# Recurrent mixer with five gate projections one iteration earlier and modulation rows in its last iterations; both MLPs with the second product's first weights loaded third

## The chip, the cores and the metric

The kernel runs on one core of a Trainium2 chip. The metric is the device time of one execution in microseconds (us); the time before is the median of three runs. One further execution was recorded by the hardware profiler, and all rows below are from it. The engines are PE (matrix products), DVE, ACT, POOL and SP; in this kernel SP only issues transfers, and POOL issues some and does a few sums.

## The reference, cut to what matters

The kernel computes a trunk of two layers on one sequence of 1024 frames and 1024 channels. Layer A is a recurrent mixer and an MLP, layer B an attention and an MLP. The change touches the mixer and both MLPs:

```python
def recurrent_mixer(hn, w_in, ...):
    z = hn @ w_in                                  # 1024 -> 2 x 1408
    gate, xr = jnp.split(z, 2, axis=-1)
    xr = causal_depthwise_conv(xr, conv_w, conv_b) # width 4
    y = rg_lru(xr, ...)                            # 16 blocks of 88 channels
    return (y * jax.nn.gelu(gate)) @ w_out
...
    r = sigmoid(einsum(xb, w_a) + b_a); i = sigmoid(einsum(xb, w_x) + b_x)
    log_a = -8.0 * r * softplus(-lam); a = exp(log_a)
    u = sqrt(-expm1(2.0 * log_a)) * (i * x)
    h[s] = a[s] * h[s - 1] + u[s]                  # along the sequence
...
def sqrelu_mlp(hn, w1, w2):
    return jnp.square(jax.nn.relu(hn @ w1)) @ w2
...
    mod = c_act @ ada_w[layer] + ada_b[layer]      # six vectors that modulate a layer
```

## The kernel before, in words

**Products.** Every product is made in three passes (`mm3`, L329 to L331) from operands that are split into a high part (a rounded copy, made by ACT, L196) and a low part (the rest, made by DVE, L200): low part by weights' high, high by weights' low, high by high. So each weight and each operand costs an ACT and a DVE instruction before PE can use it.

**The stream.** A planner (`Stream`) holds one list of all weights, modulation rows and MLP operands. `load` sends the transfers in the list's order through SP's queue (L159) into seven staging slots (`ws`); a slot comes free when its last split has run. Instructions are emitted in program order, with a hand-made clock of *ticks*: `at(d, f)` puts a job d ticks later. A projection unit (`proj2`) has four ticks, a block of `gates` one. Each engine works through its own instructions strictly in the order in which they were emitted.

**The mixer.** `w_in` gives 22 units of 128 channels: 11 of `xr` (unit t) and 11 of `gate` (unit 11 + t). A unit is 48 matmuls: two halves of 512 frames by 8 chunks by 3 passes. `xr(t)` runs a unit; ACT scales it into two tiles (L912, L914); `conv(t)` is three DVE steps (L919). One tick later `copies` moves the rows of tile t into tiles of one 88-channel block each by transfers that POOL issues (L927); `split_hi` (ACT, L933) and `split_lo` (DVE, L940) follow after 5 and 6 ticks for tiles 3 to 9. `_done(t)` lists the blocks that are complete with tile t: 4 is [5, 6], 7 is [10], 8 is [11, 12]. `recur` runs the blocks of a tile: `gates` (12 matmuls of 88 rows each, sigmoids on ACT, L966; the product i·x on DVE, L971), `tanhs` and `roots` (ACT, the last step is L986), and for each block `scan` and `scan2` on DVE (L990, L991, L992, L996, L997). `ycopy` sends the result to tiles of 128 channels (POOL, L1004), `gated` multiplies it with the GELU of the gate (DVE, L1010), and SP stores it. Iteration t of the loop (4 to 10) is `xr(t)`, `recur(_done(t - 1))`, `gate(t - 1)`. So PE goes: ... xr 4, block 4, gate 3, xr 5, blocks 5 and 6, gate 4, xr 6, block 7, gate 5, ... xr 8, block 10, gate 7, xr 9, blocks 11 and 12, gate 8, xr 10, block 13, gate 9, gate 10, blocks 14 and 15.

**Modulation rows.** `some(n)` puts n rows of `ada_w` into the list. Each is one load of 512 KB and one DVE instruction (L362) that reduces it into a vector.

**The MLPs.** Both products go by seven products for each 2 by 2 block (`PROD`: B11, T1, T2, B22, B21, T3, T4 name the combinations of the hidden operand; `quads.step` runs them). The first product's results are stored to `hid` by ACT's queue, their differences are formed on DVE (L1174), and the second product reads them back as operands. Its weights come as *quads*: four loads of 256 KB in three of the seven slots, four sums on DVE (L126; on POOL from the third quad on), then the splits. At its first step (`s == 0`) the list holds six loads of operands (B11, T1 and T2, two loads each), then the first quad, then the other operands. The results are added into `h` on DVE (L1278), which frees the bank; L1256 adds in the first product.

Of the kernel before, what the change touches and what calls it, by code (L numbers as in the profile page):

```python
# [18 lines left out]
NT = 11  # L19
# [284 lines left out]
def trunk(ctx: ExitStack, tc: tile.TileContext, I, out, dbg=None, stop=None):  # L304
# [103 lines left out]
    gate_item(_done(0) + _done(1))  # L408
    w_in(2)
    gate_item(_done(2))  # L410
    for t in range(4, NT):
        w_in(NT + t)
        some({4: 3, 6: 3, 8: 2}.get(t, 0))
        gate_item(_done(t - 1))
        w_in(t - 1)
    w_in(NT - 1)
    gate_item(_done(NT - 1))
    ygd = dp.tile([NT, 128, S], F32, name="ygd")
# [55 lines left out]
    def mlp_units(l):  # L474
        for f in range(4):
            ws.add(I["w1"][l][f], 1024)
        for q in range(2, 16):
            u, v = I["w1"][l][2 * q], I["w1"][l][2 * q + 1]
            ws.add_quad(u[:, :512], u[:, 512:], v[:, :512], v[:, 512:], 512, V)
            ada_late(0 if l or q == 2 else 2 if q in (3, 15) else 3)  # L480
        for s in STEPS[: 16 if l else 15]:
            c = slice(s * 128, s * 128 + 512)
            if s == 0:

                for nm in NAMES[:3]:
                    hid_item(l, [(0, nm), (1, nm)])
                    hid_item(l, [(2, nm), (3, nm)])
            ws.add_quad(*(I["w2"][l][s % 4][x][:, c] for x in range(4)), 512, G if s > 1 else V)
            if s == 0:
                for nm in NAMES[3:]:  # L490
                    hid_item(l, [(0, nm), (1, nm)])
                    hid_item(l, [(2, nm), (3, nm)])
            if l or s < 14:
                if s < 15:
                    for nms in HLOADS:
                        hid_item(l, [(s + 4, nm) for nm in nms])
        if l == 0:
            for e in range(2):
                ws.add(I["w2t"][e], 1024)
            hid_item(l, [(18, "B11"), (18, "B12")])  # L500
            hid_item(l, [(18, "B22"), (18, "B21")])
            hid_item(l, [(16, "B12"), (17, "B12")])
            hid_item(l, [(15, "B12")])
# [392 lines left out]
    at = ws.at  # L896
# [47 lines left out]
    def conved(t):  # L944

        conv(t)
        at(1, copies, t)
        late = 2 < t < NT - 1
        at(5 if late else 3, split_hi, t)
        at(6 if late else 4, split_lo, t)  # L950

    gunit = [None]

# [106 lines left out]
    recur(_done(0) + _done(1))  # L1060
    gate(2)
    recur(_done(2))
    for t in range(4, NT):
        xr(t)
        recur(_done(t - 1))
        gate(t - 1)
    ws.cap["a"] = 14
    gate(NT - 1)
    recur(_done(NT - 1))
# [739 lines left out]
```

## Time and profile before

| | us |
|---|---|
| median of 3 runs (lowest to highest) | 2373.84 (2373.54 to 2380.44) |
| the profiled execution | 2376.3 |
| its span | 2374.5 |
| PE busy | 2276.8 (96%) |
| DVE busy | 1751.4 (74%) |
| ACT busy | 1242.1 (52%) |
| mean granted clock of PE | 0.988 of full |

PE is busy for nearly the whole span, so the time follows PE: it is the sum of PE's work at the clock that was granted, and of its idle time. The rows below are read in this way: a view of 50 us stretches shows where PE is idle or slow, the waits name who ended the idle time, and the timelines of the other engines show why that one was late. The granted clock is 1.00 at 2.4 GHz and 0.50 at 1.2 GHz; a stretch with both has a mean between. "Busy" of PE is longer at half the clock for the same work.

### The profile page before, as it was taken

How to read it: one execution, taken by the hardware profiler on the slowest of the kernel's cores; microseconds unless marked ns; L12 is line 12 of the kernel's file. 1: busy time of each engine (PE TensorE's matmuls, PEld its weight loads, DVE VectorE, ACT ScalarE, POOL GpSimd, SP SyncE). 2: the span in 40 equal slices, each digit the busy share in tenths (PEclk: the TensorE clock that was granted, in tenths of full speed). 3: DMA queues.
4: the chain of work that ended last, by engine and by line, in shares of the span. 5: the costliest groups of instructions: out<-in, count | busy, mean ns of one | idle time of the engine just before them, and what ended most of it. 6: DMA issues, size and time to landing. Idle time of an engine off the chain costs nothing.

```text
span 2374.5 us, 31723 instructions
## 1 busy us (share of the span) xinstructions
PE 2276.8 (96%) x11740; PEld 1932.3 (81%) x11740; DVE 1751.4 (74%) x2580; ACT 1242.1 (52%) x2051; POOL 398.9 (17%) x419
## 2 busy tenths in 40 slices
PE   4998999999999899999999999999999999999999
PEld 2876777878887677888999999998888888778887
DVE  8687779588787777777774638997386665777775
ACT  5596783275554533434433229996175555634342
POOL 0000100000000023330000048874000000033322
PEclk9998999999999999999999999999999999999999
DMA  8333339326666865546344200014214444865543
GB/s 317 93 110 118 112 110 345 115 72 239 239 246 228 287 236 150 157 140 223 109 141 134 80 10 13 10 43 138 76 40 177 160 160 171 292 236 161 153 148 135
DMA packets 141639, 363.46 MB, mean 153 GB/s; under 512 B 14924, under 2 KB 17100, under 8 KB 141484
## 3 DMA queue, kind: packets, MB, share of 16 engines
q1 hardware_dynamic: 113756, 278.45, 35.2%
q10 hardware_dynamic: 23824, 71.44, 8.0%
q0 software_dynamic: 3904, 11.54, 1.9%
q8 instruction: 92, 1.51, 0.3%
q14 instruction: 63, 0.52, 0.1%
HBM read 260.19 MB, written 89.65 MB: 147 GB/s over the span
## 4 chain that ended last, share of the span: by engine, by line
PE 66%; DVE 11%; DMA 10%; ACT 7%; issue 4%; POOL 1%; ACTq 0%; SPq 0%; DVEq 0%; POOLq 0%
PE b L330 20%; PE b L331 20%; PE b L329 20%; DMA hid<-s 5%; DMA ws<-in_w_dram 3%; DVE wl L200 2%; PE b L1615 2%; ACT s L1585 1%; DVE s L200 1%; DVE s L1174 1%; ACT s L334 1%; DMA ws<-hid 1%; POOL ws L126 1%; PE b L1634 1%; PE b L1635 1%
## 5 line engine op out<-in xcount | busy, mean ns | idle before, releaser
L329 PE MATMUL b<-s,wh 128*128 128x512 f32 (+1 forms) x2532 | 1000.5, 395 | 33.9 <-DVE s L1278 7.1
L330 PE MATMUL b<-s,wh 128*128 128x512 f32 (+1 forms) x2532 | 995.4, 393 | 19.3 <-DVE s L940 10.4
L331 PE MATMUL b<-s,wl 128*128 128x512 f32 (+1 forms) x2296 | 903.3, 393 | 4.7 <-DVE wl L200 4.7
L329 PEld LDWEIGHTS b<-s,wh 128*128 128x128 f32 (+1 forms) x2532 | 478.3, 189 | 150.3 <-ACT wh L196 10.0
L330 PEld LDWEIGHTS b<-s,wh 128*128 128x128 f32 (+1 forms) x2532 | 478.5, 189 | 125.3 <-DVE s L940 10.8
L196 ACT ACTIVATE wh<-ws 128x1024 fp32r<-128x1024 f32 (+2 forms) x302 | 290.7, 972 | 481.7 <-POOL ws L126 250.2
L331 PEld LDWEIGHTS b<-s,wl 128*128 128x128 f32 (+1 forms) x2296 | 434.1, 189 | 101.7 <-DVE wl L200 7.5
L200 DVE TENSOR_TENSOR wl<-ws,wh 128x1024 fp32r<-128x1024 f32 (+2 forms) x249 | 304.8, 1227 | 133.3 <-ACT wh L196 131.1
L1278 DVE SCALAR_TENSOR_TENSOR s<-b,mod,s 128x512 f32<-128x512 f32 x221 | 164.5, 745 | 86.3 <-PE b L331 86.2
L200 DVE TENSOR_TENSOR s<-ws,s 128x512 fp32r<-128x512 f32 x284 | 224.2, 807 | 0.0
L126 POOL TENSOR_TENSOR ws<-ws 128x512 f32<-128x512 f32 x21 | 27.7, 1319 | 1144.7 <-DMA s<-hsp 463.8
L329 PE MATMUL b<-wh,s 128*128 128x256 f32 x768 | 216.5, 284 | 0.0
L331 PE MATMUL b<-wh,s 128*128 128x256 f32 x768 | 215.2, 283 | 0.9 <-DVE s L580 0.9
L330 PE MATMUL b<-wl,s 128*128 128x256 f32 x768 | 215.9, 283 | 0.0
L196 ACT ACTIVATE s<-ws 128x512 fp32r<-128x512 f32 x284 | 164.0, 618 | 55.0 <-DMA ws<-hid 22.2
L331 PEld LDWEIGHTS b<-wh,s 128*128 128x128 f32 x768 | 146.5, 192 | 1.4 <-DVE s L580 1.3
L329 PEld LDWEIGHTS b<-wh,s 128*128 128x128 f32 x768 | 147.1, 192 | 0.3 <-issue 0.2
L330 PEld LDWEIGHTS b<-wl,s 128*128 128x128 f32 x768 | 147.0, 192 | 0.3 <-issue 0.2
L362 DVE CUSTOM_DVE_ANT_0 ws<-ws,cb,vec 128x1024 f32<-128x1024 f32 x59 | 75.2, 1280 | 74.9 <-DMA ws<-in_ada_dram 72.2
L1256 DVE TENSOR_TENSOR s<-s,b 128x512 f32<-128x512 f32 x84 | 57.3, 683 | 73.4 <-PE b L331 66.9
L1254 ACT ACTIVATE s<-b 128x512 f32<-128x512 f32 x84 | 50.1, 596 | 90.5 <-PE b L331 89.3
L1385 ACT ACTIVATE s<-b 128x256 f32<-128x256 f32 x96 | 31.6, 387 | 122.4 <-PE b L331 110.8
(165 smaller groups left out, 3066.3 us busy)
## 6 DMA issues: line engine op xcount, KB each, us to landing
hid<-s ACTq DMA_DIRECT2D x128, 512.0 KB, 5.1
ws<-hid SPq DMA_DIRECT2D x118, 512.0 KB, 4.8
ws<-in_w_dram SPq DMA_DIRECT2D x220, 256.0 KB, 3.7
ws<-in_ada_dram SPq DMA_DIRECT2D x56, 512.0 KB, 4.4
s<-in_ada_dram SPq DMA_DIRECT2D x40, 512.0 KB, 9.1
ws<-in_w_in_dram SPq DMA_DIRECT2D x22, 512.0 KB, 5.9
hsp<-s SPq DMA_DIRECT2D x32, 256.0 KB, 2.0
s<-hsp SPq DMA_DIRECT2D x16, 512.0 KB, 6.3
```

The source lines that it names most:

```text
L126: eng.tensor_tensor(out=out, in0=in0, in1=in1, op=op)
L196: self.nc.scalar.activation(out=hi[:rows, :n], in_=src, func=AF.Copy)
L200: self.nc.vector.tensor_tensor(out=lo[:rows, :n], in0=src, in1=hi[:rows, :n].bitcast(F32), op=ALU.subtract)
L329: PE.matmul(ps, ah, bh, start=start, stop=False, skip_group_check=more)
L330: PE.matmul(ps, ah, bl, start=False, stop=False, skip_group_check=more)
L331: return PE.matmul(ps, al, bh, start=False, stop=stop, skip_group_check=more).ins
L362: V.tensor_tensor_reduce(out=t, in0=t, in1=cb, op0=ALU.mult, op1=ALU.add, scale=1.0, scalar=bias, accum_out=dst)
L1254: A_.activation(out=t, in_=ps, func=AF.Copy)
L1256: V.tensor_tensor(out=t, in0=t, in1=ps, op=ALU.add)
L1278: V.scalar_tensor_tensor(out=t, in0=ps, scalar=g2[:, m : m + 1], in1=t, op0=ALU.mult, op1=ALU.add)
L1385: A_.activation(out=d, in_=ps[:, :, e * 128 : (e + 1) * 128], func=AF.Copy)
L1615: PE.transpose(ps[:, x, e * 128 : (e + 1) * 128], ptile[e][:, col : col + 128], ident)
```

## The change

**The mixer.** The unit `gate(3)` runs ahead of the loop, and iteration t runs `gate(t)` for t = 4 to 7 (tiles 3 to 7, five units, each one iteration earlier), none at t = 8, and `gate(t - 1)` at t = 9 and 10 as before. The list of weights follows. The splits of the converted rows come after 4 and 5 ticks instead of 5 and 6, and after 3 and 4 for tile 8. The modulation rows are listed at iterations 8, 9 and 10 (3, 2, 3) instead of 4, 6 and 8 (3, 3, 2).

**The MLPs.** At `s == 0` the first quad stands behind the two loads of B11, ahead of those of T1 and T2.

```diff
@@ the list of weights, mixer
     w_in(2)
     gate_item(_done(2))
+    w_in(3)
     for t in range(4, NT):
         w_in(NT + t)
-        some({4: 3, 6: 3, 8: 2}.get(t, 0))
+        some({8: 3, 9: 2, 10: 3}.get(t, 0))
         gate_item(_done(t - 1))
-        w_in(t - 1)
+        if t != 8:
+            w_in(t if t < 8 else t - 1)
@@ mlp_units
             if s == 0:
 
-                for nm in NAMES[:3]:
+                for nm in NAMES:
                     hid_item(l, [(0, nm), (1, nm)])
                     hid_item(l, [(2, nm), (3, nm)])
-            ws.add_quad(*(I["w2"][l][s % 4][x][:, c] for x in range(4)), 512, G if s > 1 else V)
-            if s == 0:
-                for nm in NAMES[3:]:
-                    hid_item(l, [(0, nm), (1, nm)])
-                    hid_item(l, [(2, nm), (3, nm)])
+                    if nm == "B11":
+                        quad(0)
+            else:
+                quad(s)
@@ conved
-        late = 2 < t < NT - 1
-        at(5 if late else 3, split_hi, t)
-        at(6 if late else 4, split_lo, t)
+        late = 2 < t < NT - 1 and t != 8
+        at(4 if late else 3, split_hi, t)
+        at(5 if late else 4, split_lo, t)
@@ the loop
     recur(_done(2))
+    gate(3)
     for t in range(4, NT):
         xr(t)
         recur(_done(t - 1))
-        gate(t - 1)
+        if t != 8:
+            gate(t if t < 8 else t - 1)
```

In the changed kernel the lines that are named here stand five or seven further down: L919 is L924, L933 is L938, L940 is L945, L971 is L976, L990 to L992 are L995 to L997, L996 and L997 are L1001 and L1002, L1010 is L1015.

**First place: DVE ahead of the low splits of blocks 5 and 6.** Before (the two L940 rows read the blocks' tiles s_1135 and s_1138; L990 to L997 are the scan of block 4, L200 the low split of a weight, L1010 is `gated`):

```order
L1010 TENSOR_TENSOR s_704<-s_704,s_1045 128x1024
L990 SCALAR_TENSOR_TENSOR s_1116<-s_1085,s_1116 88x1024
L991 SCALAR_TENSOR_TENSOR s_1085<-s_1085,s_1114 88x1024
L992 TENSOR_SCALAR s_1085<-s_1085 88x1024
L996 TENSOR_TENSOR s_1116<-s_1116,s_856 88x1024
L997 SCALAR_TENSOR_TENSOR s_1114<-s_1085,s_1116 88x1024
L200 TENSOR_TENSOR wl_1212<-ws_777,wh_1211 128x1024
L940 TENSOR_TENSOR s_1233<-s_1135,s_1207 88x1024
L940 TENSOR_TENSOR s_1235<-s_1138,s_1209 88x1024
```

Now (s_1184 and s_1187 are the tiles of blocks 5 and 6; L924 is the convolution of tile 4, from which they are copied, L976 the i·x of block 4):

```order
L924 SCALAR_TENSOR_TENSOR s_1094<-s_1093,vec,s_1094 128x1023
L924 SCALAR_TENSOR_TENSOR s_1094<-s_1093,vec,s_1094 128x1022
L924 SCALAR_TENSOR_TENSOR s_1094<-s_1093,vec,s_1094 128x1021
L200 TENSOR_TENSOR wl_1162<-ws_748,wh_1161 128x1024
L976 TENSOR_TENSOR s_847<-s_1140,s_847 88x1024
L995 SCALAR_TENSOR_TENSOR s_1168<-s_1139,s_1168 88x1024
L996 SCALAR_TENSOR_TENSOR s_1139<-s_1139,s_1166 88x1024
L997 TENSOR_SCALAR s_1139<-s_1139 88x1024
L945 TENSOR_TENSOR s_1252<-s_1184,s_1229 88x1024
L945 TENSOR_TENSOR s_1254<-s_1187,s_1231 88x1024
L1001 TENSOR_TENSOR s_1168<-s_1168,s_847 88x1024
L1002 SCALAR_TENSOR_TENSOR s_1166<-s_1139,s_1168 88x1024
```

The two low splits have moved from behind the last two steps of block 4's scan and a weight's low split to between its third and fourth steps.

**Second place: DVE ahead of the low splits of blocks 11 and 12.** Before, from the second step of tile 8's convolution on (L990 to L997 are the scan of block 10, s_1712 its tile; the L940 rows read s_1911 and s_1914, the tiles of blocks 11 and 12):

```order
L919 SCALAR_TENSOR_TENSOR s_1821<-s_1820,vec,s_1821 128x1022
L919 SCALAR_TENSOR_TENSOR s_1821<-s_1820,vec,s_1821 128x1021
L200 TENSOR_TENSOR wl_1889<-ws_1398,wh_1888 88x704
L971 TENSOR_TENSOR s_1712<-s_1867,s_1712 88x1024
L990 SCALAR_TENSOR_TENSOR s_1895<-s_1866,s_1895 88x1024
L991 SCALAR_TENSOR_TENSOR s_1866<-s_1866,s_1893 88x1024
L992 TENSOR_SCALAR s_1866<-s_1866 88x1024
L996 TENSOR_TENSOR s_1895<-s_1895,s_1712 88x1024
L997 SCALAR_TENSOR_TENSOR s_1893<-s_1866,s_1895 88x1024
L200 TENSOR_TENSOR wl_1980<-ws_1461,wh_1979 128x1024
L940 TENSOR_TENSOR s_2001<-s_1911,s_1975 88x1024
L940 TENSOR_TENSOR s_2003<-s_1914,s_1977 88x1024
```

Now, from the last step of block 9's scan on (s_1764 is the tile of block 10, s_1970 and s_1973 are those of blocks 11 and 12):

```order
L1002 SCALAR_TENSOR_TENSOR s_1772<-s_1742,s_1776 88x1024
L1015 TENSOR_TENSOR s_1444<-s_1444,s_1678 128x1024
L924 SCALAR_TENSOR_TENSOR s_1880<-s_1879,vec,s_1880 128x1023
L924 SCALAR_TENSOR_TENSOR s_1880<-s_1879,vec,s_1880 128x1022
L924 SCALAR_TENSOR_TENSOR s_1880<-s_1879,vec,s_1880 128x1021
L200 TENSOR_TENSOR wl_1948<-ws_1595,wh_1947 128x1024
L976 TENSOR_TENSOR s_1764<-s_1926,s_1764 88x1024
L945 TENSOR_TENSOR s_2025<-s_1970,s_2007 88x1024
L945 TENSOR_TENSOR s_2027<-s_1973,s_2009 88x1024
L995 SCALAR_TENSOR_TENSOR s_1954<-s_1925,s_1954 88x1024
```

The two low splits have moved from behind the scan of block 10 and a second weight split to right behind block 10's i·x; between tile 8's convolution and them two instructions of DVE are left of eight. On PE the unit `gate(7)`, which stood between xr 8 and these blocks, is gone from there.

**Third place: SP at the start of the first MLP's second product.** Before (one row per load; x2 is two):

```order
L159 DMA ws_5527<-hid 128x2x512
L159 DMA ws_5569<-hid 128x2x512
L159 DMA ws_5573<-hid 128x2x512
L159 DMA ws_5613<-hid 128x2x512
L159 DMA ws_5663<-hid 128x2x512
L159 DMA ws_5703<-hid 128x2x512
L159 DMA ws_5707<-in_w_dram 128x512
L159 DMA ws_5740<-in_w_dram 128x512
L159 DMA ws_5763<-in_w_dram 128x512 x2
L159 DMA ws_5770<-hid 128x2x512
```

Now:

```order
L159 DMA ws_5527<-hid 128x2x512
L159 DMA ws_5569<-hid 128x2x512
L159 DMA ws_5573<-in_w_dram 128x512
L159 DMA ws_5662<-in_w_dram 128x512
L159 DMA ws_5702<-in_w_dram 128x512 x2
L159 DMA ws_5707<-hid 128x2x512
L159 DMA ws_5735<-hid 128x2x512
L159 DMA ws_5741<-hid 128x2x512
L159 DMA ws_5769<-hid 128x2x512
L159 DMA ws_5773<-hid 128x2x512
```

The four loads of weights have moved from the seventh place to the third, and the four loads of T1's and T2's operands behind them. DVE's instructions follow: the sums and the splits of the first weights now stand ahead of the low splits of T1 and T2. The second MLP has the same pieces in the same order.

## Rows read from the trace of the kernel before

**Rows 1.** The page, part 1: busy time, share of the span and instructions of PE.

```profile
PE 2276.8 (96%) x11740; PEld 1932.3 (81%) x11740; DVE 1751.4 (74%) x2580; ACT 1242.1 (52%) x2051; POOL 398.9 (17%) x419
```

**Rows 2.** Stretches of 50 us: busy time and instructions of PE, weight loads, DVE, ACT and POOL; then the granted clock of PE, the share that the transfer engines were busy, and GB/s.

```profile
150.00:200.00 50.00, 39.63 (x149) 30.01 (x148) 45.58 (x39) 35.51 (x43) 6.33 (x12) 0.80 0.46 137
800.00:850.00 50.00, 41.23 (x146) 31.61 (x147) 43.75 (x65) 27.91 (x46) 0.26 (x1) 0.83 0.88 314
```

**Rows 3.** Waits of PE over the whole span: who ended them, us in total, times, and the longest.

```profile
PE b L330 <- DVE s L940: 10.4, 1, 10.4
...
PE b L329 <- ACT wh L196: 7.0, 4, 2.8
PE b L329 <- ACT s L196: 5.7, 2, 2.9
...
PE b L331 <- DVE wl L200: 4.7, 5, 1.4
```

**Rows 4.** Timeline of PE in the mixer, start and duration of single matmuls (a matmul starts before the one ahead of it has ended), and in brackets the idle time ahead and its releaser.

```profile
169.67 0.39 PE L330 MATMUL b<-s,wh 128*128 128x512 f32 x1
...
174.20 0.40 PE L329 MATMUL b<-s,wh 88*88 88x512 f32 x1
184.98 0.73 PE L330 MATMUL b<-s,wh 88*88 88x512 f32 x1 [10.37 <-DVE s L940]
```

**Rows 5.** The stretch behind that wait, columns as in rows 2.

```profile
185.00:197.50 12.50, 12.50 (x30) 8.36 (x31) 11.08 (x11) 8.01 (x11) 0.55 (x1) 0.50 0.68 211
```

**Rows 6.** Timelines of ACT and DVE: the high splits of blocks 5 and 6, the end of block 1's scan, and the low splits of blocks 5 and 6 (start, duration).

```profile
168.49 2.01 ACT L933 ACTIVATE s<-s 88x1024 fp32r<-88x1024 f32 x2
...
150.25 2.29 DVE L997 TENSOR_TENSOR_SCAN s<-s,s 88x1024 f32<-88x1024 f32 x1
...
183.71 2.35 DVE L940 TENSOR_TENSOR s<-s,s 88x1024 fp32r<-88x1024 f32 x2
```

**Rows 7.** Timelines of ACT and DVE from the gates of blocks 8 and 9 to the convolution of tile 8.

```profile
248.54 2.42 ACT L966 ACTIVATE s<-b,vec 88x512 f32<-88x512 f32 x4
...
257.65 2.19 ACT L986 ACTIVATE s<-s,sp 88x1024 f32<-88x1024 f32 x2
259.75 1.04 ACT L933 ACTIVATE s<-s 88x1024 fp32r<-88x1024 f32 x1
...
258.84 1.22 DVE L990 SCALAR_TENSOR_TENSOR s<-s,s 88x1024 f32<-88x1024 f32 x1 [6.63 <-ACT s L986]
...
261.95 1.22 DVE L940 TENSOR_TENSOR s<-s,s 88x1024 fp32r<-88x1024 f32 x1
...
267.67 1.22 DVE L990 SCALAR_TENSOR_TENSOR s<-s,s 88x1024 f32<-88x1024 f32 x1
...
274.24 1.20 DVE L1010 TENSOR_TENSOR s<-s,s 128x1024 f32<-128x1024 f32 x1
275.35 3.91 DVE L919 SCALAR_TENSOR_TENSOR s<-s,vec,s 128x1023 f32<-128x1023 f32 x3
279.18 0.88 DVE L200 TENSOR_TENSOR wl<-ws,wh 88x704 fp32r<-88x704 f32 x1
```

**Rows 8.** The copies of blocks 11 and 12: their issue on POOL, and the transfers issued from 279 to 281 (KB each, us from issue to landing).

```profile
279.83 1.02 POOL L927 DMA_DIRECT2D s<-s  x2 [3.93 <-issue]
...
s<-s POOLq DMA_DIRECT2D x1, 352.0 KB, 5.7
s<-s POOLq DMA_DIRECT2D x1, 128.0 KB, 3.5
```

**Rows 9.** The first MLP at the start of its second product: timelines of SP (time from the first issue to the end of the last of a row), DVE and PE.

```profile
763.28 25.94 SPq L159 DMA_DIRECT2D ws<-hid  x6
789.46 4.48 SPq L159 DMA_DIRECT2D ws<-in_w_dram  x4
...
789.35 4.90 DVE L200 TENSOR_TENSOR s<-ws,s 128x512 fp32r<-128x512 f32 x8
799.61 0.69 DVE L126 TENSOR_TENSOR ws<-ws 128x512 f32<-128x512 f32 x1 [5.37 <-DMA ws<-in_w_dram]
...
816.34 0.74 DVE L1278 SCALAR_TENSOR_TENSOR s<-b,mod,s 128x512 f32<-128x512 f32 x1
...
801.45 0.62 PE L329 MATMUL b<-s,wh 128*128 128x512 f32 x1 [2.81 <-ACT wh L196]
...
817.23 0.47 PE L329 MATMUL b<-s,wh 128*128 128x512 f32 x1 [2.93 <-ACT s L196]
...
831.90 0.50 PE L329 MATMUL b<-s,wh 128*128 128x512 f32 x1 [1.90 <-ACT wh L196]
```

**Rows 10.** Stretches there, columns as in rows 2.

```profile
801.45:808.50 7.05, 6.00 (x14) 4.20 (x15) 7.02 (x11) 6.29 (x11) 0.00 (x0) 0.52 0.90 299
...
806.00:831.00 25.00, 20.90 (x78) 16.02 (x76) 22.25 (x35) 15.03 (x27) 0.00 (x0) 0.88 0.94 334
```

**Rows 11.** The second MLP at the same place: timelines of DVE and PE, and one stretch.

```profile
2042.44 0.69 DVE L126 TENSOR_TENSOR ws<-ws 128x512 f32<-128x512 f32 x1 [2.26 <-DMA ws<-in_w_dram]
...
2059.17 0.74 DVE L1278 SCALAR_TENSOR_TENSOR s<-b,mod,s 128x512 f32<-128x512 f32 x1
...
2060.06 0.47 PE L329 MATMUL b<-s,wh 128*128 128x512 f32 x1 [2.81 <-ACT s L196]
...
2048.00:2072.00 24.00, 21.19 (x87) 17.06 (x86) 22.35 (x36) 15.64 (x28) 0.00 (x0) 0.93 0.96 342
```

More of the change, by code (lines that the diff above doesn't have):

```diff
@@ L481, in mlp_units, with quad @@
         for s in STEPS[: 16 if l else 15]:
-            c = slice(s * 128, s * 128 + 512)
+            def quad(s):
+                c = slice(s * 128, s * 128 + 512)
+                ws.add_quad(*(I["w2"][l][s % 4][x][:, c] for x in range(4)), 512,
+                            G if s > 1 else V)
             if s == 0:
-                for nm in NAMES[:3]:
+                for nm in NAMES:
                     hid_item(l, [(0, nm), (1, nm)])
                     hid_item(l, [(2, nm), (3, nm)])
-            ws.add_quad(*(I["w2"][l][s % 4][x][:, c] for x in range(4)), 512, G if s > 1 else V)
-            if s == 0:
-                for nm in NAMES[3:]:
-                    hid_item(l, [(0, nm), (1, nm)])
-                    hid_item(l, [(2, nm), (3, nm)])
+                    if nm == "B11":
+                        quad(0)
+            else:
+                quad(s)
             if l or s < 14:
```

## The prediction

> **What bounds the kernel now.** The page's first part comes first: PE is busy for 2276.8 of 2374.5 us [rows 1], so a change of this size can only gain where PE is idle or slow. The 50 us stretches then show two such places that the change touches: 150 to 200, where PE has 39.63 us of work at a mean clock of 0.80, and 800 to 850, with 41.23 at 0.83 [rows 2]. The waits of PE say who ended the idle time: in the mixer one wait of 10.4 us on a low split (L940); in the MLPs the high splits of weights (7.0 in four waits), the low splits of weights (4.7 in five) and the high splits of operands (5.7 in two) [rows 3].
>
> *The mixer.* PE's first matmul of block 5 starts at 174.20, the second, which reads the low part, at 184.98 [rows 4]. From 185.0 to 197.5 the clock is 0.50 and PE is busy for all of 12.50 us [rows 5]: at the full level that work is 6.25 us, so the wait costs 10.37 + 6.25 = **16.6 us**. The high splits were done at 170.5, the low ones began at 183.71 [rows 6]: DVE, which runs its list in order, was still at older scans. Its backlog is the cause, not data that came late.
>
> *The MLPs.* In the first one PE waits 2.81 us ahead of B11, 2.93 ahead of T2 and 1.90 ahead of the second quad [rows 9]. Behind the first of these the mean clock is 0.52 over 7.05 us [rows 10], some 3.4 us lost. DVE sat idle for 5.37 us until the last load of the first quad had landed (799.61) [rows 9].
>
> **The mixer, step by step.** A unit of 48 matmuls takes 10.9 us: 20 of them start in 4.53 us (169.67 to 174.20) [rows 4]; the 12 of a block take 2.7. PE takes up xr 4 at about 138.6 (counted back from 174.20 by xr 5, gate 3, block 4 and xr 4). In its place comes `gate(3)`, whose weights now stand at xr 4's place in the list, so they come when xr 4's came. Counting on from 138.6: gate 3 to 149.5, xr 4 to 160.4, block 4 to 163.1, gate 4 to 174, xr 5 to **185**. Blocks 5 and 6 are wanted 10.8 us later than before.
>
> *When are they ready?* Block 1's scan ends at 152.5 [rows 6]; ahead of its end the order is nearly the same. DVE then has, up to the end of tile 4's convolution: two scans of 6.57 (267.67 to 274.24), two `gated` of 1.1, two weight splits of 1.1 and a convolution of 3.83 [rows 7]: 152.5 + 13.1 + 2.2 + 2.2 + 3.8 = 173.8. The copies follow 0.65 later on POOL (279.18 to 279.83) and land after 3.5 to 5.7 [rows 7, 8]; a high split is 1.04 and a low split 1.1 [rows 7]. Together: 180 to 182. Slack is 3 to 5 us, so the stall and its slow clock should go: **+16.6**. The moved modulation rows help here, as none stands ahead of these splits now; I put them at nothing elsewhere: in DVE's new list they lie between blocks 5 and 6 and block 8's scan, a stretch in which DVE had gaps (the last of 6.63 us before 258.84 [rows 7]). If that cover failed, eight of some 1.3 would cost up to 10.
>
> *What is next.* One gate unit is now ahead, and it is used up at tile 8, whose iteration has none. PE after: blocks 8 and 9 from 236.9 to 242.4 (5.7 earlier than before), gate 7 to 253.3, xr 8 to 264.2, block 10 to 266.9, xr 9 to **277.8**; then blocks 11 and 12. Before, `gate(7)` stood between and blocks 11 and 12 were not wanted until 294. DVE's list leads to them in one chain: block 9's sigmoids and exponentials shift by 5.7, so block 8's exponential is done at 258.84 − 5.7 = 253.1; block 9's and the high split of tile 7's block end at 260.8 − 5.7 = 255.1, and its low split (261.95, formerly inside block 8's scan) now stands ahead of that scan: 256.2 [rows 7]. Two scans 13.1, a weight split of 0.8, `gated` 1.1 and tile 8's convolution 3.83 end at 275.1. Copies issued at 275.8; block 11's second piece lands 3.5 later at 279.3, block 12 5.7 later, at 282.1 [rows 8]. High split 1.05, low split 1.1: 281.4 against 278 wanted, a **new stall of 3.4**. Block 12 follows 2.7 us behind and is just in time. The stall of 2.81 was followed by 3.4 us of loss to the slow clock [rows 9, 10], though with another of 1.05 behind it; I take half of that, 1.7. So 5.1 is given back: mixer **+11.5**, between 16.6 (copies quicker, or ACT ahead) and 3 (stall near 8 us, with 5 to 6 of slow clock).
>
> **The MLPs, step by step.** *First MLP, B11.* Staging slots come free one by one from 763.28 to about 789; six loads of operands took them, and the four of weights went out from 789.46 to 793.94 [rows 9]. Now the weights take the third to sixth slot, so the last goes out at about 789.4, some 4.5 earlier, and no earlier, for the sixth slot is the late one. Sums start at 794 to 795; PE's B11 needs the high split 1.84 later (799.61 to 801.45) [rows 9], at 796.6, when PE is still busy (it ran out at 801.45 − 2.81 = 798.64). The wait, the 1.05 behind it for the low split, and 3.4 of slow clock go: 7.3. *But* T2 waits for the bank that L1278 at 816.34 frees, and DVE is busy without a break from 799.61 to there, 16.7 us. The eight low splits of T1's and T2's operands, 4.90 us that ran at 789.35 while DVE was waiting anyway [rows 9], now come behind the sums: 794.3 + 16.7 + 4.9 = 815.9. T2 starts only about 1 us earlier; most of the 7.3 becomes waiting ahead of T1 and T2. What follows waits for the second quad (1.90), whose loads wait for slots that these splits free: 1 to 3 us earlier. First MLP **+2**, from −1 (the longer wait brings a longer slow clock) to +6 (splits find other gaps). *Second MLP.* No wait at B11: DVE's sums ran from 2042.44 after an idle 2.26, in time; the wait is at T2 (2.81, after L1278 at 2059.17) [rows 11]. The sums move forward by what the eight splits move back, so L1278 stays: **0**, from −4 to +1.5.
>
> *A rule against this part.* From 806 to 831 the transfer engines are busy to 94% and move 334 GB/s, and in the second MLP from 2048 to 2072 342 GB/s [rows 10, 11]; there, another order of the same loads brings one operand earlier and another later. The Trainium skill (DMA: Bandwidth & Descriptors, section Bandwidth) gives about 358 GB/s as one core's limit to and from HBM; by that rule the order alone gains nothing where this rate is reached, and the trace is close to it in both stretches. By it both MLPs would be 0.
>
> **Sum.** 11.5 + 2 + 0 = 13.5. The profiled execution took 2376.3, so 2362.8 by its own time; the median of the runs is 2.5 below it, so I forecast **2360**.
>
> **The rivals.**
> *No new stall at block 11.* The chain needs only 3.4 us less: for it speaks that each landing and ACT's place is estimated; against it that DVE's list is full from 256 on. 16.6 + 2 = 18.6: 2355.
> *The MLPs gain nothing or lose.* By the transfer limit, or by the late operands: 11.5 + 0 − 0 to 4, 2362 to 2366. For it: T2's wait depends on DVE's sum of work, which is not less.
> *The stall moves to blocks 11 and 12.* A wait near 8 with some 6 of slow clock (10.37 brought 6.25) leaves 16.6 − 14 + 2 = 4.6: 2369. For it: the same chain, with one later landing or one more weight split in it.
> *Slower.* The last moved modulation row (L362) stands on DVE right ahead of tile 7's low split and block 8's scan. DVE runs in order, so if its load is late by x beyond its cover, the whole chain to blocks 11 and 12 is late by x, at 1.6 us of PE for each (10.37 + 6.25 over 10.37). The cover is about 8 us (i·x of block 9 to the exponentials, idle 6.63 before [rows 7]). It decides from x near 8: at 13, 16.6 + 2 − 1.6 × (3.4 + 13) = −7.6, that is 2381. Against it: in DVE's new list the instruction that frees its slot stands twelve ahead.
>
> **How the numbers follow.** Forecast (a stall of 1 to 6 us at block 11) 0.55, all of it faster; no stall 0.17; MLPs without gain 0.15, faster by 7.5 to 11.5; stall moved 0.09, within 0.3%; slower 0.04. A difference of 0.3%, 7.1 us, is what a measurement can tell from none. Rounding for the edges: faster 0.83, same 0.13, slower 0.04. The range runs from 16.6 + 6 (2351) to the stall that is nearly moved (2369).
>
> **What would show it.** Right: no wait on L945 near 185 and the clock 1.00 from 150 to 260; a wait of 2 to 5 us on L945 behind xr 9 near 278; PE's last block at about 340 instead of 352; no wait on a high split at B11 in the first MLP, and longer ones ahead of T1 or T2. Wrong: a wait on L945 or on a weight split at blocks 5 and 6 (slack misjudged), one over 8 us behind xr 9, or T2 later than 817.23 − 11.5.

## The result and the profile after

The changed kernel takes 2363.05 us (median of five runs, 2361.46 to 2366.05) against 2374.08 for the one before (five runs, 2373.54 to 2380.44). The ratio is 0.9946 with an interval of 0.9929 to 0.9964, so it is faster by 0.5%, some 11 to 13 us. The profiled execution is the one of 2363.05 us, with a span of 2361.2.

The 50 us stretches of the changed kernel (columns as in rows 2) answer to [rows 2]; 250 to 300 is added:

```profile
150.00:200.00 50.00, 50.00 (x221) 40.02 (x221) 45.24 (x38) 38.65 (x47) 6.29 (x12) 1.00 0.48 141
...
250.00:300.00 50.00, 46.83 (x179) 35.44 (x178) 42.65 (x37) 41.08 (x49) 5.75 (x11) 0.86 0.36 103
...
800.00:850.00 50.00, 45.39 (x183) 35.05 (x183) 42.64 (x61) 26.25 (x43) 6.33 (x4) 0.95 0.86 303
```

Before, 250 to 300 was full:

```profile
250.00:300.00 50.00, 50.00 (x222) 40.03 (x221) 39.23 (x32) 38.84 (x46) 4.62 (x9) 1.00 0.34 102
```

The stretch from 150 to 200 has no idle time and no slow clock left (39.63 at 0.80 before). 800 to 850 is better (45.39 at 0.95 against 41.23 at 0.83). But 250 to 300 is now the poor one: 46.83 us of busy time at a mean clock of 0.86.

The waits of PE (as rows 3) show the same:

```profile
PE b L329 <- DVE s L1285: 12.5, 10, 2.8
PE b L329 <- DVE s L1263: 9.4, 5, 4.4
...
PE b L331 <- DVE wl L200: 2.9, 3, 1.4
...
PE b L329 <- ACT s L938: 2.5, 1, 2.5
...
PE b L329 <- ACT wh L196: 1.3, 2, 0.7
...
PE b L330 <- DVE s L945: 0.6, 1, 0.6
```

The 10.4 us on the low split of block 5 are gone. Waits on high splits of weights fell from 7.0 to 1.3, on low splits of weights from 4.7 to 2.9. In their place stand banks (places that hold PE's results until DVE has read them) that DVE has to read (L1263 and L1285, 21.9 in 15 waits; the same lines, L1256 and L1278, had 4.1 and 7.1), and block 11: 2.5 on its high split and 0.6 on its low split. The 5.7 on the high splits of operands (L196) are gone only in part: ahead of T2 in the second MLP PE still waits 2.82, which the profile now puts down to L1285.

Where the time came from is seen by taking the start of the same matmul in both traces (the n-th that PE ran; the mixer's order differs, so the places below lie between its units). The table gives by how many us each kernel is ahead of before there; the kernels of the experiments, told below, stand beside it.

| place (time in before) | changed | mixer alone | MLPs alone | gate 8 first | ticks as before | same, timed | scan 9 last (with `gated` later) |
|---|---|---|---|---|---|---|---|
| behind blocks 5 and 6 (200) | 14.9 | 15.4 | 0.4 | 15.9 | 16.2 | 13.4 | 12.9 |
| ahead of blocks 11 and 12 (268) | 14.8 | 14.9 | 0.4 | 12.2 | 15.1 | 13.2 | 12.8 |
| behind them (314) | 5.3 | 5.8 | 0.4 | 10.1 | 13.2 | 11.2 | 11.2 |
| output projection (398) | 8.2 | 5.8 | 0.5 | 7.9 | 13.1 | 11.3 | 3.9 |
| first MLP, late in its first product (733) | 8.0 | 5.6 | 0.0 | 7.1 | 10.0 | 8.0 | 1.2 |
| first MLP, second product's early quads done (918) | 14.4 | 6.4 | 10.4 | 16.8 | 18.8 | 15.6 | 12.1 |
| second MLP, ahead of T1 (2041) | 14.4 | 5.0 | 10.7 | 17.7 | 17.9 | 12.8 | 11.7 |
| second MLP, some quads later (2201) | 13.3 | 4.6 | 9.7 | 17.5 | 17.4 | 12.2 | 10.4 |

So in the changed kernel the mixer gains 15, gives 9.5 of it back at blocks 11 and 12, gets 2.7 more by the time of the first MLP, and the first MLP adds 6.5. Single traces of one kernel differ by a few us (the two of "ticks as before" by 2.8 as early as 200 and by 5.2 at the end), so only differences above that are read from single traces.

**Block 11.** Timelines of ACT, DVE, POOL and PE of the changed kernel (the rows that answer to [rows 7, 8]):

```profile
257.11 1.04 ACT L938 ACTIVATE s<-s 88x1024 fp32r<-88x1024 f32 x1
...
281.18 1.06 ACT L938 ACTIVATE s<-s 88x1024 fp32r<-88x1024 f32 x1 [2.14 <-DMA s<-s]
...
258.19 1.22 DVE L945 TENSOR_TENSOR s<-s,s 88x1024 fp32r<-88x1024 f32 x1 [2.91 <-ACT s L938]
259.33 1.21 DVE L995 SCALAR_TENSOR_TENSOR s<-s,s 88x1024 f32<-88x1024 f32 x1
...
274.37 3.91 DVE L924 SCALAR_TENSOR_TENSOR s<-s,vec,s 128x1023 f32<-128x1023 f32 x3
...
282.27 1.22 DVE L945 TENSOR_TENSOR s<-s,s 88x1024 fp32r<-88x1024 f32 x1 [1.72 <-ACT s L938]
...
278.86 1.04 POOL L932 DMA_DIRECT2D s<-s  x2 [3.92 <-ACT s L917]
...
282.29 0.62 PE L329 MATMUL b<-s,wh 88*88 88x512 f32 x1 [2.53 <-ACT s L938]
283.55 0.73 PE L330 MATMUL b<-s,wh 88*88 88x512 f32 x1 [0.64 <-DVE s L945]
```

The stretch behind the wait, columns as in rows 2:

```profile
282.45:296.10 13.65, 13.02 (x31) 8.25 (x31) 11.21 (x10) 10.97 (x15) 0.54 (x1) 0.50 0.13 32
```

The chain is the one that was summed. DVE sits idle for 2.91 us until ACT has made tile 7's high split (257.11 to 258.15), does the low split, and only then begins block 8's scan (259.33). Tile 8's convolution ends at 278.2, the copies go out at 278.86, block 11's high split starts on landing, and PE starts its second matmul at 283.55, after 2.53 + 0.64 = 3.17 us of waiting. Then the clock is 0.50 for 13.65 us, in which PE is busy for 13.02: 31 matmuls.

**First MLP.** Timelines of SP, DVE and PE (these answer to [rows 9]; before's times less 8.0 are comparable):

```profile
754.30 7.89 SPq L159 DMA_DIRECT2D ws<-hid  x2
762.42 7.20 SPq L159 DMA_DIRECT2D ws<-in_w_dram  x4
777.14 15.49 SPq L159 DMA_DIRECT2D ws<-hid  x8
...
780.04 0.69 DVE L126 TENSOR_TENSOR ws<-ws 128x512 f32<-128x512 f32 x1
...
804.52 0.74 DVE L1285 SCALAR_TENSOR_TENSOR s<-b,mod,s 128x512 f32<-128x512 f32 x1
...
815.82 0.69 DVE L126 TENSOR_TENSOR ws<-ws 128x512 f32<-128x512 f32 x1 [1.26 <-DMA ws<-in_w_dram]
...
799.54 0.80 PE L329 MATMUL b<-s,wh 128*128 128x512 f32 x1 [4.42 <-DVE s L1263]
...
805.41 0.47 PE L329 MATMUL b<-s,wh 128*128 128x512 f32 x1 [0.48 <-DVE s L1285]
...
817.65 0.50 PE L329 MATMUL b<-s,wh 128*128 128x512 f32 x1 [0.75 <-ACT wh L196]
...
819.76 0.50 PE L331 MATMUL b<-s,wl 128*128 128x512 f32 x1 [1.37 <-DVE wl L200]
```

Two stretches there (as [rows 10]):

```profile
797.86:804.69 6.83, 5.15 (x12) 3.80 (x12) 6.73 (x11) 4.67 (x9) 0.00 (x0) 0.50 1.04 395
817.60:824.00 6.40, 4.98 (x21) 3.82 (x22) 6.37 (x9) 4.61 (x8) 0.00 (x0) 1.00 0.72 220
```

The four loads of weights go out from 762.42 to 769.62 (770.4 to 777.6 on before's clock, where they went out from 789.46 to 793.94). DVE makes the sums at 780.04 without having waited for them. PE's wait ahead of B11 is gone; one of 4.42 stands where a bank must be read (L1263) and brings 6.83 us of slow clock. T2 starts after 0.48 us and not 2.93. What T2 waits for is less sure than the prediction has it: before, the profile names ACT's high split as the releaser [rows 9], and L1278 ended within 0.2 us of PE's start as well. In the changed kernel both came about 4 us earlier on the common clock, so which of the two decides isn't shown. The second quad is there at 817.65, 6.3 earlier on the common clock than 831.90, and the clock stays at 1.00 behind it.

### The profile page after: what moved, and what is told of

Its sections match the earlier page's. It is cut to its first block, busy times and chain, and to the rows that moved or that the text cites. A ratio compares the mean times of both kernels' runs of the same rounds, so it can differ in the third digit from the quotient of the medians.

```text
span 2361.2 us, 31725 instructions
## 1 busy us (share of the span) xinstructions
PE 2272.8 (96%) x11740; PEld 1929.1 (82%) x11740; DVE 1749.7 (74%) x2580; ACT 1240.2 (53%) x2051; POOL 399.2 (17%) x419
## 4 chain that ended last, share of the span: by engine, by line
PE 63%; DVE 9%; DMA 8%; ACT 7%; issue 3%; POOL 1%; ACTq 0%; SPq 0%; DVEq 0%; POOLq 0%
PE b L329 20%; PE b L331 20%; PE b L330 20%; DMA hid<-s 2%; DMA ws<-in_w_dram 2%; DMA ws<-hid 2%; ACT s L1592 2%; PE b L1622 1%; DVE wl L200 1%; ACT s L334 1%; DVE s L200 1%; PE b L1641 1%; PE b L1642 1%; DMA s<-s 1%; DVE s L1181 1%
## 5 line engine op out<-in xcount | busy, mean ns | idle before, releaser
L329 PE MATMUL b<-s,wh 128*128 128x512 f32 (+1 forms) x2532 | 999.7, 395 | 36.7 <-DVE s L1285 12.5
L331 PE MATMUL b<-s,wl 128*128 128x512 f32 x2296 | 901.1, 392 | 2.9 <-DVE wl L200 2.9
L329 PEld LDWEIGHTS b<-s,wh 128*128 128x128 f32 (+1 forms) x2532 | 477.4, 189 | 153.2 <-DVE s L1263 11.5
L196 ACT ACTIVATE wh<-ws 128x1024 fp32r<-128x1024 f32 (+3 forms) x302 | 290.7, 972 | 474.7 <-POOL ws L126 266.7
L331 PEld LDWEIGHTS b<-s,wl 128*128 128x128 f32 x2296 | 432.8, 189 | 98.0 <-DVE wl L200 4.6
L200 DVE TENSOR_TENSOR wl<-ws,wh 128x1024 fp32r<-128x1024 f32 (+1 forms) x249 | 303.0, 1220 | 136.4 <-ACT wh L196 134.0
L200 DVE TENSOR_TENSOR s<-ws,s 128x512 fp32r<-128x512 f32 x284 | 226.1, 812 | 8.1 <-ACT s L196 8.1
L1285 DVE SCALAR_TENSOR_TENSOR s<-b,mod,s 128x512 f32<-128x512 f32 x221 | 164.5, 745 | 77.5 <-PE b L331 77.2
L196 ACT ACTIVATE s<-ws 128x512 fp32r<-128x512 f32 x284 | 164.2, 618 | 58.3 <-DMA ws<-hid 27.0
L362 DVE CUSTOM_DVE_ANT_0 ws<-ws,cb,vec 128x1024 f32<-128x1024 f32 x59 | 75.1, 1280 | 70.3 <-DMA ws<-in_ada_dram 67.4
L1263 DVE TENSOR_TENSOR s<-s,b 128x512 f32<-128x512 f32 x84 | 57.2, 682 | 73.6 <-PE b L331 61.6
```

What stands on the lines that cost most here:

```text
L196: self.nc.scalar.activation(out=hi[:rows, :n], in_=src, func=AF.Copy)
L200: self.nc.vector.tensor_tensor(out=lo[:rows, :n], in0=src, in1=hi[:rows, :n].bitcast(F32), op=ALU.subtract)
L329: PE.matmul(ps, ah, bh, start=start, stop=False, skip_group_check=more)
L331: return PE.matmul(ps, al, bh, start=False, stop=stop, skip_group_check=more).ins
L362: V.tensor_tensor_reduce(out=t, in0=t, in1=cb, op0=ALU.mult, op1=ALU.add, scale=1.0, scalar=bias, accum_out=dst)
L1263: V.tensor_tensor(out=t, in0=t, in1=ps, op=ALU.add)
```

## The experiments

Times are medians, with the ratio to the runs of the kernel before on the same chip where there was an interval; other kernels have one run.

**Each part alone.** *The mixer's part, with the list of the MLPs as before:*

```diff
# against the changed kernel, in mlp_units at s == 0
-                for nm in NAMES:
+                for nm in NAMES[:3]:
                     hid_item(l, [(0, nm), (1, nm)])
                     hid_item(l, [(2, nm), (3, nm)])
-                    if nm == "B11":
-                        quad(0)
+            ws.add_quad(...)               # as before, behind six loads of operands
```

> The mixer's part alone, both MLPs in the order of before. Theory (the trace of the changed kernel: 15 us ahead of before at blocks 5 and 6, 5.3 ahead behind blocks 11 and 12, 8 to 9 ahead at the start of the first MLP): about 8 to 9 us faster than before, near 2365, with a wait of 3 us and 13 us at half the clock behind xr 9. Rival (the MLPs give nothing, and what the trace shows there is the mixer's lead seen later): 11 to 13 us faster, near 2362.

Measured: 2368.2, ratio 0.9975 (0.9964 to 0.9986), 5.9 us faster. In the trace 5.6 at 733 and 4.6 at the end. A wait of 3.1 + 0.8 at block 11 is there.

*The MLPs' part, with the mixer as before:*

```diff
# against the kernel before, in mlp_units at s == 0, both MLPs
-                for nm in NAMES[:3]:
+                for nm in NAMES:
                     hid_item(l, [(0, nm), (1, nm)])
                     hid_item(l, [(2, nm), (3, nm)])
+                    if nm == "B11":
+                        quad(0)
```

> The MLPs' part alone, the mixer as before. Theory: the first MLP gives 5 to 6 us, the second loses about 1: 4 to 5 us faster than before, near 2369, with the wait of 10.4 us at block 5 still there. Rival (transfers near their limit, so that the order gives nothing): within 2 us of before.

Measured: 2367.83, ratio 0.9970 (0.9960 to 0.9979), 7.1 us faster; in the trace 10.4 in the first MLP and 1.0 lost in the second. The stretch there, columns as in rows 2:

```profile
800.00:850.00 50.00, 43.66 (x179) 33.96 (x177) 42.83 (x62) 27.71 (x46) 6.34 (x4) 0.97 0.90 331
```

By ratios the parts are worth 5.9 and 7.1, together 13.0, and the changed kernel 12.8: they add up. Which of the two is larger can't be told, since the intervals (3.3 to 8.5 and 5.0 to 9.5 us) overlap. The mixer's share came out below the 8 to 9 of its theory, and that of the MLPs above its 4 to 5.

**What makes block 11 late.** *Block 9's scan behind tile 8's convolution (four ticks later):*

```diff
-            at(3 + 2 * n, scan, b)
+            at(9 if b == 9 else 3 + 2 * n, scan, b)
```

> The changed kernel with the scan of block 9 four ticks later, so that on DVE it stands behind tile 8's convolution and not ahead of it. Theory (that scan, 6.6 us, is what makes the copies of blocks 11 and 12 late): copies go out about 6 us earlier, no wait at block 11, clock 1.00 from 250 to 300, 10 us faster than the changed kernel, near 2353. Rival (the landing time of the copies or ACT's place decides): the wait stays over 2 us and the time within 3 us of the changed kernel.

Measured: 2362.18, ratio 0.9947 (0.9932 to 0.9962), no better than the changed kernel. The copies went out 3.2 us earlier, but the wait at block 11 grew to 4.78, for the scan now stood between them and the low splits. DVE:

```profile
276.10 1.22 DVE L995 SCALAR_TENSOR_TENSOR s<-s,s 88x1024 f32<-88x1024 f32 x1
...
281.60 2.29 DVE L1002 TENSOR_TENSOR_SCAN s<-s,s 88x1024 f32<-88x1024 f32 x1
283.81 2.33 DVE L945 TENSOR_TENSOR s<-s,s 88x1024 fp32r<-88x1024 f32 x2
```

The theory's size failed, and the rival's reason too: the landing did not decide, DVE's order did.

*Block 9's scan behind the low splits of blocks 11 and 12, without and with tile 5's `gated` behind the convolution:*

```diff
-            at(3 + 2 * n, scan, b)
+            at(13 if b == 9 else 3 + 2 * n, scan, b)
# in the second kernel only
-                at(2, gated, u)
+                at(4 if u == 5 else 2, gated, u)
```

> The changed kernel with the scan of block 9 behind the low splits of blocks 11 and 12, and the product of tile 5 with its gate where the changed kernel has it. It tells whether the wait of 6.6 us at block 14 in the run that moved both came from that product or from DVE's backlog. Theory (DVE has the same work and the copies of the last tile wait behind it): a wait of 0 to 2 us at block 11, one of 4 us or more at blocks 14 and 15 or behind gate 10, the time within 4 us of the changed kernel. Rival (the product's later store bunched the splits ahead of the last GELU): no wait over 1.5 us at block 14, and 6 to 10 us faster than the changed kernel, near 2355.

> The changed kernel with the scan of block 9 moved behind the low splits of blocks 11 and 12 on DVE, and the product of tile 5 with its gate (it waited 2.85 us for a transfer, ahead of tile 8's convolution) behind that convolution. Theory (in the run with that scan between the convolution and the low splits the copies did go out 3.2 us earlier, but the low splits then waited for the scan; without it they follow the copies): tile 8's convolution ends near 271, low split of block 11 near 278, wait at block 11 under 1 us, the clock 1.00 there, PE 14 to 15 us ahead of before behind blocks 11 and 12 and not 5; 8 to 10 us faster than the changed kernel, near 2354. Rival (the landing of the copies decides): a wait of 2 us or more stays and the time is within 4 us of the changed kernel.

Measured: 2367.6 (0.9954, 0.9936 to 0.9971) and 2364.41 (0.9946, 0.9929 to 0.9962). Both have no more than 0.8 us of wait at block 11 and PE still 11 to 12 ahead behind blocks 11 and 12, and both lose it ahead of block 14. ACT and PE of the second one:

```profile
333.63 1.06 ACT L938 ACTIVATE s<-s 88x1024 fp32r<-88x1024 f32 x1 [11.30 <-DMA s<-s]
...
340.06 7.38 ACT L196 ACTIVATE s<-ws 128x512 fp32r<-128x512 f32 x14
347.34 1.06 ACT L911 ACTIVATE s<-b 128x512 f32<-128x512 f32 x2
...
347.97 0.73 PE L329 MATMUL b<-s,wh 88*88 88x512 f32 x1 [6.60 <-ACT s L911]
```

ACT waits 11.3 us for the copies of the last tile, whose convolution now stands behind the delayed scans, then does 14 splits of other operands, and only then the GELU that frees PE's bank: a wait of 6.6 with 10.2 us of slow clock. The backlog was moved, not removed. `gated` had no part in it.

*The unit gate 8 ahead of blocks 11 and 12 (weights likewise):*

```diff
+        if t == 9:
+            gate(8)
         recur(_done(t - 1))
-        if t != 8:
+        if t not in (8, 9):
             gate(t if t < 8 else t - 1)
```

> The changed kernel with one unit placed otherwise: in the iteration of tile 9 the unit gate 8 runs ahead of blocks 11 and 12 and not behind them (its weights are listed ahead of theirs too). Theory (what is given back is the wait at block 11 and the slow clock behind it, 3.2 and 6.8 us): no wait there, 10 us faster than the changed kernel, near 2353. Rival (the backlog on DVE only moves on): a wait of similar size at block 13 or at blocks 14 and 15, and a time within 3 us of the changed kernel.

Measured: 2360.77, ratio 0.9942 (0.9927 to 0.9957). The wait at block 11 is gone, and PE is 10.1 ahead behind it and not 5.3; but only 7.1 at 733, no more than the changed kernel's 8.0. So there is no gain that can be told from none, and half of the theory failed. Other waits stand in its trace instead: 1.81 at 301.04 and 2.64 at 355.4 on low splits of weights, the second with 3.41 us at half the clock, so the lead is partly given up elsewhere, as the rival said.

*The ticks of before (5 and 6) for tiles 3 to 7 and 9; tile 8 as changed:*

```diff
-        at(4 if late else 3, split_hi, t)
-        at(5 if late else 4, split_lo, t)
+        at(5 if late else 3, split_hi, t)
+        at(6 if late else 4, split_lo, t)
```

> The changed kernel with the splits of tiles 3 to 7, 9 at 5 and 6 ticks again (tile 8 as changed). Theory (block 5's and 6's splits had 3 to 5 us of slack, so one tick later on DVE costs little): a wait of 0 to 2 us at blocks 5 and 6, time within 4 us of the changed kernel. Rival (the earlier ticks are what removes the wait): a wait of over 4 us there with slow clock behind it, 6 us or more slower than the changed kernel.

> The kernel with the ticks of before for all tiles but tile 8 once more, now timed. Theory (the earlier tick put tile 7's low split ahead of block 8's scan, where DVE sat idle for 2.9 us until ACT's high split; that is the 3.2 us by which block 11 came late, and 6.8 of slow clock followed): wait at block 11 under 1.5 us, PE 12 to 14 us ahead of before behind blocks 11 and 12, and 4 to 8 us faster than the changed kernel, a ratio to before of 0.991 to 0.993. Rival (the one run was a lucky one): a ratio of 0.994 to 0.996, as the changed kernel.

Measured: one run of 2358.93, then, timed, 2359.66 with a ratio of 0.9926 (0.9915 to 0.9938). PE waits 0.8 on the low split at block 11 in both traces, and 0.8 at blocks 5 and 6 in the first of them alone; the clock stays at 1.00 at both places. So the earlier ticks are not what removed the wait at blocks 5 and 6. DVE in the first of the two traces, then the stretch:

```profile
254.62 1.22 DVE L995 SCALAR_TENSOR_TENSOR s<-s,s 88x1024 f32<-88x1024 f32 x1 [5.03 <-ACT s L991]
...
257.74 1.22 DVE L945 TENSOR_TENSOR s<-s,s 88x1024 fp32r<-88x1024 f32 x1
...
279.76 1.22 DVE L945 TENSOR_TENSOR s<-s,s 88x1024 fp32r<-88x1024 f32 x1 [2.77 <-ACT s L938]
```

```profile
250.00:300.00 50.00, 48.84 (x213) 38.31 (x212) 40.28 (x33) 42.85 (x51) 5.22 (x10) 1.00 0.34 95
```

Block 8's scan now starts as soon as its exponential is done, and tile 7's low split runs inside it. In this trace ACT was also 1.6 us earlier than in the changed kernel (its last step ahead of the scan began at 253.44 against 255.01), so the start at 254.62 is not the order's work alone. In the second trace that step began at 255.29, later than in the changed kernel, and the scan still began 2.9 us before 259.33:

```profile
256.47 1.22 DVE L995 SCALAR_TENSOR_TENSOR s<-s,s 88x1024 f32<-88x1024 f32 x1 [3.85 <-ACT s L991]
...
259.59 1.22 DVE L945 TENSOR_TENSOR s<-s,s 88x1024 fp32r<-88x1024 f32 x1
```

So the earlier tick, a part of the change, is what made block 11 late: it put an instruction that waits for ACT ahead of the chain. The edit moved the splits of all these tiles; that tile 7's is the one that counts is read from DVE's order, and no run moved it alone. This kernel has the best ratio of the study, 0.2% ahead of the changed one, though the two intervals overlap a little. Behind blocks 11 and 12 its two traces are 6 to 8 us ahead of the changed kernel's; some 3 us of that are lost near 475 (told below).

*The modulation rows where they were:*

```diff
-        some({8: 3, 9: 2, 10: 3}.get(t, 0))
+        some({4: 3, 6: 3, 8: 2}.get(t, 0))
```

> The changed kernel with the modulation rows listed at the iterations of tiles 4, 6 and 8 as before. Theory (without them DVE reaches the low splits of blocks 5 and 6 in time, by a slack of 3 to 5 us): two or three rows of 1.3 us and what they wait for lie ahead of those splits again; a wait of 0 to 3 us at blocks 5 and 6 and, with the slow clock behind it, a time up to 8 us above the changed kernel. Rival (they don't matter for it): no wait there, and at block 11 a shorter one, since two rows fewer stand ahead of block 8's scan.

Measured: 2361.43 in one run. There is no wait on a low split at blocks 5 and 6, and 2.2 + 0.8 at block 11, as the rival said, though shorter by 0.2 only. In this run the place of the rows doesn't matter for blocks 5 and 6.

**How long the slow clock lasts.** *Gate 8 between blocks 11 and 12 (weights likewise, and no gate 8 behind them):*

```diff
         for b in bs:
             gates(b)
+            if b == 11:
+                gate(8)
```

> The changed kernel with the unit gate 8 between blocks 11 and 12 (its weights listed ahead of those blocks'), so that behind the wait PE runs 12 matmuls of 88 rows and then 48 of 128 rows, and not 24 of 88 rows. Theory (the slow clock ends only when matmuls of 128 rows run again: 13.65 us of it in the changed kernel cover the 24 small ones at 0.43 each and 1.7 us more): the wait of about 3 us at block 11 stays, the slow stretch is 7 to 10 us. Rival (its length follows from the wait alone): 13.65 us again, 7 of them in gate 8.

*The kernel with gate 8 first, and one added instruction on DVE (so it does that much more; what it computes is the same):*

```diff
+        if t == 8:
+            lo = it["lo"][:, 0:128]
+            V.tensor_scalar(out=lo, in0=lo.bitcast(F32), scalar1=1.0, scalar2=0.0,
+                            op0=ALU.mult, op1=ALU.add)
```

> The kernel with gate 8 ahead of blocks 11 and 12, in which PE doesn't wait behind xr 9, plus one small DVE instruction that writes 128 columns of gate 8's low weights over themselves (times 1) behind tile 9's convolution, so that PE waits some 5 to 6 us there, and then has 48 matmuls of 128 rows, not 24 of 88. Theory (behind a wait the slow clock ends once PE runs matmuls of 128 rows: 11.8 to 13.8 us from the wait's end to the full clock with 24 small ones behind it in five traces, 9.7 with 12): 4 to 7 us from the wait's end to the full clock. Rival (it follows from the wait's length alone): 12 us or more, as after the waits of 3.2 and 4.8.

Measured: the first 2360.92 and the second 2378.3, one run each. Stretches from the end of the wait to the full clock, columns as in rows 2; first the one with gate 8 between, then the one with the wait ahead of gate 8:

```profile
284.40:294.10 9.70, 9.13 (x21) 6.11 (x22) 7.99 (x8) 7.79 (x10) 0.00 (x0) 0.50 0.04 11
```

```profile
284.10:295.12 11.02, 0.00 (x0) 0.00 (x0) 9.44 (x10) 4.60 (x6) 0.00 (x0) 0.50 0.04 10
295.12:301.17 6.05, 6.05 (x14) 4.79 (x15) 4.59 (x4) 0.00 (x0) 1.59 (x3) 0.50 0.35 79
```

| kernel | wait, us | behind it | from its end to full clock, us |
|---|---|---|---|
| before, block 5 | 10.37 | 23 matmuls of 88 rows | 12.5 |
| changed, block 11 | 3.17 | 24 of 88 | 13.8 |
| scan 9 later | 4.78 | 23 of 88 | 11.8 |
| gate 8 between | 3.86 | 12 of 88, then 128 | 9.7 |
| wait ahead of gate 8 | 13.51 | 128 only | 6.05 |

In the changed kernel and the one with gate 8 between, the wait is two waits close together; counted from the end of the second, their last column is 12.5 and 8.4.

The added instruction made a wait of 13.51, not 5 to 6, and the longest wait has the shortest slow stretch behind it. That speaks against the wait's length as what sets the stretch. In every row with small matmuls the slow clock outlasts them; the 24 small ones take 24 × 0.427 = 10.2 us at half the clock. But that the kind of matmul is the cause isn't shown, and another place of the same traces speaks against it as the whole of the cause. Near 475, at the start of the first MLP, every one of the fourteen traces has a wait of 3.44 to 3.46 us. Behind it PE runs the same list in all: eight matmuls of 128 by 128, eight that give one column each, then more of 128 by 128. The changed kernel, then the first one with the ticks of before:

```profile
476.47 0.50 PE L330 MATMUL b<-s,wh 128*128 128x512 f32 x1 [3.45 <-DVE s L624]
...
477.01:480.42 3.41, 3.41 (x12) 2.78 (x10) 2.47 (x4) 0.00 (x0) 0.00 (x0) 0.50 0.35 108
```

```profile
471.59 0.79 PE L330 MATMUL b<-s,wh 128*128 128x512 f32 x1 [3.45 <-DVE s L624]
...
470.72:480.96 10.24, 9.37 (x26) 7.73 (x27) 6.83 (x15) 1.68 (x4) 0.00 (x0) 0.50 0.17 60
```

The slow stretch was 3.41 us long in six traces, 6.83 in two, 10.24 in five, and the one with gate 8 between had none. So the same wait and the same list brought anything from 0 to 10.24 us at half the clock, with no matmul of 88 rows in it. The 9.7 and the 6.05 of the table are from one trace each, and they differ by less than that. The stretches with 23 or 24 small ones lasted 11.8 us or more from the wait's end, and none near 475 more than 9.4. What sets the length stays open. That the rows of a matmul are what counts, and not something else that the gates do (each small product is short and its result is read at once), was not separated either.

**The second MLP.** *Only the first MLP's list changed:*

```diff
+                    if nm == "B11" and l == 0:
+                        quad(0)                # second MLP: quad(0) behind T2, as before
```

> The changed kernel with the second MLP's list as before (weights behind six operand loads). Theory (in the second MLP the new place costs 1.2 us, of which 1.7 are 3.4 more us at half the clock): 1 to 2 us faster than the changed kernel, near 2361.5; the wait of 2.06 at the bank ahead of T1 is gone. Rival (equal): within 0.5 us, or slower by up to 2.

Measured: 2360.7, ratio 0.9935 (0.9920 to 0.9950), against 0.9946 (0.9929 to 0.9964): not to be told apart. In the second MLP (2041 to 2201) this kernel loses 1.3 against the trace of before, which has the same order there, and the changed one 1.2. So no worth of the weights' place can be seen in the second MLP.

## Why the prediction held, and which of its terms did not

The forecast was 2360 in a range of 2351 to 2369, faster by 13.5; measured 2363.05, faster by 11.0 (12.8 by the ratio). The sign and the whole were right. Of its terms:

- *Wait at blocks 5 and 6, 16.6:* right. No wait on L945 near 185 and the clock at 1.00; 14.9 ahead behind them. The missing 1.7 are a slow stretch of 3.41 us from 139.1, behind waits for ACT of 1.35 and 0.85; before they were 1.08 and 0.86, with none behind them. With the ticks as before, or the rows as before, this wait stays away (0.8 in one trace at most), so the order of the units is what is left to have removed it; the two were not taken back together.
- *New wait at block 11, 3.4:* right to 0.2 (3.17), in its place and by its chain, tile 7's low split ahead of block 8's scan included. That the size fits so well is partly luck. ACT's exponentials and the high split came 2.6 us earlier than before and not 5.7, so block 8's scan began at 259.33 and not at 256.2; against that, block 11's high split began 2.3 us after the issue of its copies and not 3.5, and PE was there at 279.8 and not at 278. The errors cancelled. The runs showed that the place of the low split is most of the wait: with the ticks as before 0.8 is left.
- *Slow clock behind it, 1.7:* the mis-sized term of the mixer. It was 13.65 us at half the clock, 6.8 lost. The step took half of what had followed a wait of like length in the MLP, where 128-row matmuls followed; the nearer row was [rows 5], where the same kind of blocks followed and 12.5 us were slow. Of the three other kernels with the same list and a wait of like size there, one had 13.65 us too, and two 10.24, that is 5.1 lost. So blocks 11 and 12 took 9.5 to 10 in the changed kernel and not 5.1, and the mixer gave 5.9 (alone, by ratio) and not 11.5.
- *First MLP, 2 (up to 6):* the other mis-sized term: 7.1 for both MLPs alone, none of it in the second. The failed step is "the weights take the third to sixth slot, so the last goes out at about 789.4 ... and no earlier". Four loads go into three slots, as the part on the kernel says, so they never met the late sixth slot: the last left at 769.6 (777.6 on before's clock), and the sums no longer waited for them. DVE's list then ran ahead: L1285 at 804.52 (812.5), 3.8 earlier and not 1, and the second quad 6.3 earlier and not 1 to 3, with the 3.4 us of loss that had followed it (6.83 us at 0.50 from 832.39) gone. This path is read from the trace; no run separates the earlier loads from DVE's new order.
- *Second MLP, 0:* right; T2 still waits 2.82 and the order makes no difference. That the transfers near their limit decide this was not tested by itself; in the first MLP, at a like rate from 806 to 831 [rows 10], the order did gain, because DVE and PE no longer waited for the late start ahead of that stretch. So the rival built on that rate falls there. The Trainium skill (DMA: Bandwidth & Descriptors, section Bandwidth) gives about 358 GB/s as one core's limit to and from HBM. The same section also has 425 GB/s measured for one core while the pair's other core is idle, and this kernel runs on one core. The changed kernel's row from 797.86 to 804.69 has 395 GB/s, loads and stores together: it passes the first figure and stays below the second.
- *The sum* came out near by luck: 5.6 too much in the mixer met 5 too little in the MLPs. The rival in which the stall moves to blocks 11 and 12 was half true: its price came, from a wait of 3 and not of 8. The rival by a late modulation row did not come: the last one (L362) began at 253.99 on DVE with no idle time ahead of it.

What happens between 314 and 733 was not predicted, and the traces show most of it. The 2.7 that the changed kernel gains there are waits of 0.69, 1.40 and 0.76 and a slow stretch of 3.41 us from 375.0 in before's trace, against waits of 0.60 and 1.21 and no slow stretch in its own. The 3 us that the kernel with the ticks of before loses in both of its traces are the slow stretch near 475, 10.24 us there against 3.41 in before. As the same wait and the same matmuls brought either, no part of the change can be named for it.

## What to carry to other kernels

A unit that is moved ahead covers a wait everywhere up to the place where the row of units ends; cost that place from a row with the same work behind the wait, where the trace has one, and give the slow clock a wide range: here it lasted 0 to 10.24 us behind one and the same wait. In an engine that works in order, a short instruction that waits for another engine should not stand ahead of a long chain: here 1.1 us of low split, waiting 2.9 for ACT, made PE wait 3.2 us and not 0.8, and 6.8 of loss at the slow clock followed. When loads are moved in a queue that is held by slots, count slots and not loads.

## What the runs showed of the hardware that was not expected

The granted clock fell to 0.50 behind waits of 3.17 to 13.51 us, and how long it stayed there did not follow the wait: 13.8 us from the end of the wait with 24 matmuls of 88 by 88 rows behind it, 9.7 with 12, 6.05 with only 128 by 128, though the last had the longest wait. Behind a wait of 3.45 us and one and the same list of matmuls, none of them 88 by 88, it was at 0.50 for 10.24 us in five of fourteen traces, 6.83 in two, 3.41 in six and not at all in one. Waits of 0.8 at block 11 brought no slow clock at all in the two runs that had the ticks of before.
